# A PEER layer kernel: top 16 of two token blocks made later, and gathered v rows of one block kept to five buffers

## The chip, the cores and the metric

The kernel runs on one core of a Trainium2 chip. A core has five engines that run side by side, each with its own instruction queue that is worked off in order: PE (TensorE, matmuls), DVE (VectorE), ACT (ScalarE), POOL (GpSimd, here the issuer of gathers) and SP (SyncE, here the issuer of plain transfers). The metric is device time in microseconds (us) of one launch.

## The reference

One layer on 1024 tokens of width 1024: attention and a gated MLP, whose output is added to x, then a PEER layer, and a last RMSNorm. The change touches PEER only:

```python
q = (xb @ w_q).reshape(PEER_TOKEN_BLOCK, PEER_HEADS, 2, PEER_HALF)
s = jnp.einsum('thpd,hpnd->thpn', q, sub_keys).astype(jnp.float32)
vals, idx = lax.top_k(s, K)                     # best 16 of 128 keys, per head and half
cand = vals[:, :, 0, :, None] + vals[:, :, 1, None, :]
best, flat = lax.top_k(cand.reshape(..., K * K), K)   # best 16 of 256 pairs
...
expert = i1 * PEER_KEYS + i2                    # one of 16384
g = jax.nn.softmax(best, axis=-1)
h = jnp.einsum('thkd,td->thk', w_u[expert], xb)
a = (g * jax.nn.gelu(h)).astype(xb.dtype)
return jnp.einsum('thk,thkd->td', a, w_v[expert])
```

With 8 heads and 16 picks a token uses 128 of 16384 experts.

## The kernel before

The tokens are eight blocks of 128. **The front**, up to some 1291 us, runs attention, MLP and the PEER query for pairs of blocks (the stages of PLAN). Its last stage S of a pair multiplies the queries by the keys (PE, 128x512 scores per block and c, tile ss, in PSUM) and `top` takes the best 16 of each 128 scores on DVE: MAX, MAX_INDEX, MATCH_REPLACE, MAX, MAX_INDEX (L565 to L569), 16 such units a block and four rows of scores each. `select(b)` takes the best 16 pairs, the expert numbers and the softmax, on DVE (scratch tiles sf, sb, so).

PEER itself is done in two ways. **Blocks 0, 1, 6, 7** gather: for each of 128 picks POOL issues an indirect transfer of one 128x1024 tile of rows (`fetch`, L664), of w_u (DVE takes the product sum, L685) and then of w_v (DVE adds to y, L699). I call these u rows and v rows, and v0 or v7 the v rows of block 0 or 7. The tiles come from gat (five buffers) and, for the names in MIXED, from gat2 (three) where a running count modulo 8 is 5 or more. gat2 exists only once the front's pools are closed; selects 6 and 7 (LATE) are emitted inside the dense stage and take their scratch from gat2.

**Blocks 2 to 5** are dense. In `gates` the 128 picks become a matrix over all experts: DVE makes one-hots oh2 (L626), ACT oh1 (L645, L646), PE multiplies them (pgg, L650), ACT copies to st (L651), SP writes st to DRAM (gd, L652). G1 is for blocks 2 and 3, G2 for 4 and 5. The **dense stage** then reads tokens (xl, L724, split in xh and xl by ACT L726 and DVE L727), gates gg (L750) and weights ur and vr (L757, L777), and runs 32 groups of 4 x 128 experts: PE hp (L765 to L767), gelu, y (L743 to L745). ACT and DVE split ur, vr and a into high and low parts (uh, ul; vh, vl; ah, al). Part of the output is summed in PSUM; for the rest DVE adds op to dacc twice a group (L791). The first group is group 0.

A scheduler puts the instructions of all this into one fixed order per engine when the kernel is built; gathered rows of blocks 0, 1, 6, 7 are spread between the other work, and what is not placed by the end of the dense stage comes after it.

Of the kernel before, what the change touches and what calls it, by code (L numbers as in the profile page):

```python
# [7 lines left out]
F32 = mybir.dt.float32  # L8
# [4 lines left out]
AF = mybir.ActivationFunctionType  # L13
# [5 lines left out]
P = 128  # L19
D = 1024  # L20
# [7 lines left out]
NPAIR = PH * K  # L28
# [14 lines left out]
FRONT_POOL = 1.0  # L43
WS = 3
G1B = (2, 3)
G1 = dict(st=1, o1=2, o2=3, gt=1)
G2 = dict(st=3, o1=4, o2=4, gt=2)
PLAN = "A0:34 A0:01g2 B0 Y0 D0 S0 X t0 u0 t1 A1:34201 A2:20134 M1 B1 Y1 D1 S1 A3:01234 B2 M2 t2 t3 Y2 M3 D2 B3 S2 t4 t5 G1 Y3 Z G2 D3 S3"
SEQ = "d u1 v0 v1 u6 v6 u7 v7"
LATE = {2: 6, 6: 7}  # L50
# [2 lines left out]
X4 = 2  # L53
UG = {3: 3, 4: 2}
WP = 3
MIXED = "v1 u6 v6 u7 v7"
OH2 = "d"
OH1 = "a"
TCK = dict(schedule_with_timeline_sim=True)
# [2 lines left out]
def peer_block(tc, d):  # L62
# [3 lines left out]
    with ExitStack() as ctx:  # L66
# [162 lines left out]
        def front():  # L229
# [300 lines left out]
            def stage_s(p):  # L530

                blocks = PASSES[p]
                for b in blocks:
                    vi = vip.tile([P, 2, PH, 2, K], F32, name=f"vi{b}", tag="vi")
                    S["vi", b] = (vi[:, 0], vi[:, 1].bitcast(U32))
                T = S["sT", p]
                nt = len(blocks) * P

                def query(c):

                    kt = f2.tile([P, 4, P], F32, name=f"kt{p}_{c}", tag="kt")
                    sp.dma_start(kt, d["keys"][:, c * 4:(c + 1) * 4, :])
                    ps = [accp.tile([P, 512], F32, name=f"pq{p}_{c}_{i}", tag="acc") for i in range(2)]
                    src = lambda q: d["w_q"][:, q * 2:q * 2 + 2, c * 512:(c + 1) * 512]
                    for dc, w in pieces(src, f"sc{p}_{c}", T[1] is None):
                        for q in range(4):
                            mm(ps[q // 2][:, (q % 2) * nt:(q % 2) * nt + nt], cut(w, slice(None), slice(q * P, (q + 1) * P)),
                               cut(T, slice(None), dc, slice(0, nt)), dc == 0 and q % 2 == 0, dc == DC - 1, skip_group_check=True)
                    qT = f2.tile([P, 4, PW * P], F32, name=f"sq{p}_{c}", tag="sq")
                    for q in range(0, 4, 2):  # L550
                        act.activation(qT[:, q:q + 2, :nt], ps[q // 2][:, :2 * nt].rearrange("p (a b) -> p a b", a=2), AF.Copy)
                    return kt, qT

                def top(c, kt, qT):
                    for i, b in enumerate(blocks):
                        vals, idxs = S["vi", b]
                        ps = accp.tile([P, 512], F32, name=f"ss{b}_{c}", tag="acc")
                        for q in range(4):
                            pe.matmul(ps[:, q * P:(q + 1) * P], qT[:, q, at(i)], kt[:, q, :], start=True, stop=True)
                        for q in range(4):  # L560
                            h, hf = (c * 4 + q) // 2, q % 2
                            s_ = ps[:, q * P:(q + 1) * P]
                            v_, i_ = vals[:, h, hf, :], idxs[:, h, hf, :]
                            rep = sm.tile([P, P], F32, name=f"rep{b}_{c}_{q}", tag="rep", bufs=2)
                            dve.max(v_[:, 0:8], s_)  # L565
                            dve.max_index(i_[:, 0:8], v_[:, 0:8], s_)
                            dve.match_replace(rep, v_[:, 0:8], s_, -3e38)
                            dve.max(v_[:, 8:16], rep)
                            dve.max_index(i_[:, 8:16], v_[:, 8:16], rep)  # L569

                last = None
                for c in range(4):
                    cur = c, *query(c)
                    if last:
                        top(*last)
                    last = cur
                top(*last)
# [76 lines left out]

        ring = [0]

        def fetch(b, src, ix, nm):
            k_ = ring[0] % (GAT + GAT2)
            ring[0] += 1
            if f"{src[2]}{b}" in MIXED and k_ >= GAT:  # L660
                t = gat2.tile([P, D], F32, name=f"{nm}", tag="gat2")
            else:
                t = gat.tile([P, D], F32, name=f"{nm}", tag="gat")
# [6 lines left out]
        def gather_u(b):  # L670
# [10 lines left out]
            dve.scalar_tensor_tensor(xn, x1, rs2_t[b], gr, op0=ALU.mult, op1=ALU.mult)  # L681
            h = gxn.tile([P, n], F32, name=f"h{b}", tag="h")
            for j in range(n):
                t = fetch(b, "w_u", idx[:, j:j + 1], f"u{b}_{j}")
                dve.tensor_tensor_reduce(t, t, xn, 1.0, 0.0, ALU.mult, ALU.add, h[:, j:j + 1])  # L685
            a = gxn.tile([P, n], F32, name=f"a{b}", tag="a")
            act.activation(a, h, AF.Gelu_apprx_tanh)
# [3 lines left out]
        def gather_v(b):  # L691
# [17 lines left out]
        def dense():  # L709
# [37 lines left out]
            for gi in range(NG):  # L747
# [122 lines left out]
```

## Time and profile before

| what | us |
|---|---|
| median of 3 runs (lowest, highest) | 2804.43 (2799.83, 2818.26) |
| the profiled execution's own time | 2804.69 |
| its span | 2802.8 |
| busy: PE, DVE, ACT, POOL | 2457.4, 2339.8, 1165.0, 1506.5 |
| mean DMA rate over the span | 310 GB/s |

The span is what the profile shows from the first to the last instruction; the 1.9 us around it belong to the launch. PE is busy in 88% of the span, DVE in 83%, ACT in 42% and POOL in 54%. These are averages over a front with changing bounds, a long dense stage and a tail, and a change has to be read in the stage that it touches.

### The profile page before, as it was taken

What the parts mean: (1) busy time and instruction counts of PE and PEld (TensorE: products, weight loads), DVE (VectorE), ACT (ScalarE), POOL (GpSimd) and SP (SyncE); (2) the same over time, 40 slices, a digit from 0 to 9 for tenths busy, and PEclk for the clock granted to TensorE, in tenths of its full rate; (3) what the DMA queues carried; (4) which work ended last, traced back from release to release, by engine and by line L of the source; (5) the groups of instructions that cost most, each with busy time, mean ns of one, the idle gap of its engine ahead of it and who ended that gap; (6) DMA issues with size and microseconds to landing.
All of it is one profiled execution on the core that took longest, in us unless ns stands there. A gap on an engine that the chain in (4) does not pass through costs nothing.

```text
span 2802.8 us, 33721 instructions
## 1 busy us (share of the span) xinstructions
PE 2457.4 (88%) x10764; PEld 1931.3 (69%) x10764; DVE 2339.8 (83%) x4967; ACT 1165.0 (42%) x2573; POOL 1506.5 (54%) x1139
## 2 busy tenths in 40 slices
PE   6789997996689767795999999999999999999990
PEld 5576654753457455684878878888888878888880
DVE  3449876999879999779998888888898788888898
ACT  4554332225863789896222323223232222323310
POOL 5262654447653346510666566565565577555665
PEclk9789998997789767795999999999999999999995
DMA  5155999998899679966999989999999999999998
GB/s 175 53 177 170 347 366 351 344 333 316 308 351 334 222 261 359 362 223 210 320 372 353 342 315 373 335 351 330 351 329 348 335 338 359 330 345 345 330 324 321
DMA packets 316513, 869.56 MB, mean 310 GB/s; under 512 B 26032, under 2 KB 93744, under 8 KB 312240
## 3 DMA queue, kind: packets, MB, share of 16 engines
q0 software_dynamic: 149760, 545.33, 53.1%
q1 hardware_dynamic: 166576, 322.09, 33.2%
q8 instruction: 84, 1.38, 0.2%
q14 instruction: 93, 0.76, 0.1%
HBM read 823.28 MB, written 44.04 MB: 309 GB/s over the span
## 4 chain that ended last, share of the span: by engine, by line
PE 40%; issue 16%; DVE 16%; POOL 11%; DMA 10%; ACT 6%; SPq 0%; POOLq 0%; DVEq 0%; ACTq 0%
POOL v L664 9%; PE pq L309 4%; PE hp L765 4%; PE hp L767 4%; PE hp L766 4%; DVE u L685 4%; PE y L744 3%; PE y L743 3%; PE y L745 3%; PE wo L309 3%; DVE y L699 3%; DMA v<-in_w_v_dram,idx 2%; DMA u<-in_w_u_dram,idx 2%; ACT oh L646 2%; PE wi L309 2%
## 5 line engine op out<-in xcount | busy, mean ns | idle before, releaser
L664 POOL DMA_INDIRECT v<-in_w_v_dram,idx x512 | 687.1, 1342 | 618.2 <-DVE y L699 326.9
L664 POOL DMA_INDIRECT u<-in_w_u_dram,idx x512 | 695.6, 1359 | 528.0 <-DVE h L685 235.2
L699 DVE SCALAR_TENSOR_TENSOR y<-v,a,y 128x1024 f32<-128x1024 f32 x512 | 656.2, 1282 | 36.8 <-DMA v<-in_w_v_dram,idx 24.8
L685 DVE CUSTOM_DVE_ANT_0 u<-u,xn 128x1024 f32<-128x1024 f32 x512 | 615.0, 1219 | 41.6 <-DMA u<-in_w_u_dram,idx 41.0
L765 PE MATMUL hp<-xh,uh 128*128 128x512 f32 x1024 | 402.6, 393 | 32.2 <-ACT uh L760 22.2
L767 PE MATMUL hp<-xh,ul 128*128 128x512 f32 x1024 | 400.8, 392 | 2.6 <-DVE ul L761 2.6
L766 PE MATMUL hp<-xl,uh 128*128 128x512 f32 x1024 | 401.3, 392 | 0.0
L778 ACT ACTIVATE vh<-vr 128x1024 fp32r<-128x1024 f32 x128 | 131.5, 1052 | 503.7 <-PE op L745 485.3
L650 PE MATMUL pgg<-oh,oh 128*128 128x128 f32 x1024 | 219.7, 368 | 114.3 <-ACT st L651 69.3
L743 PE MATMUL y<-vh,ah 128*128 128x512 f32 x768 | 298.8, 389 | 0.0
L744 PE MATMUL y<-vl,ah 128*128 128x512 f32 x768 | 298.8, 389 | 0.0
L650 PEld LDWEIGHTS pgg<-oh,oh 128*128 128x128 f32 x1024 | 186.9, 261 | 158.4 <-ACT st L651 81.9
L745 PE MATMUL y<-vh,al 128*128 128x512 f32 x768 | 286.1, 390 | 2.9 <-DVE al L775 2.9
L765 PEld LDWEIGHTS hp<-xh,uh 128*128 128x128 f32 x1024 | 194.2, 190 | 75.9 <-ACT uh L760 23.3
L646 ACT ACTIVATE oh<-oh,gT 128x128 f32<-128x128 f32 x512 | 221.9, 512 | 16.3 <-DVE gT L613 16.3
L767 PEld LDWEIGHTS hp<-xh,ul 128*128 128x128 f32 x1024 | 193.8, 189 | 44.0 <-DVE ul L761 3.3
L766 PEld LDWEIGHTS hp<-xl,uh 128*128 128x128 f32 x1024 | 194.1, 190 | 40.0
L760 ACT ACTIVATE uh<-ur 128x1024 fp32r<-128x1024 f32 x128 | 135.3, 1057 | 177.8 <-PE hp L766 165.5
L309 PE MATMUL pq<-sT,sc 128*128 128x256 f32 x768 | 186.0, 392 | 2.0 <-ACT sT L127 2.0
L761 DVE TENSOR_TENSOR ul<-ur,uh 128x1024 fp32r<-128x1024 f32 x128 | 156.3, 1221 | 19.9 <-ACT uh L760 19.9
L645 ACT ACTIVATE oh<-iota,gT 128x128 f32<-128x128 f32 x512 | 168.7, 420 | 7.7 <-PE pgg L650 7.6
L309 PEld LDWEIGHTS pq<-sT,sc 128*128 128x128 f32 x768 | 144.3, 195 | 34.6 <-issue 9.2
(439 smaller groups left out, 4141.3 us busy)
## 6 DMA issues: line engine op xcount, KB each, us to landing
ur<-in_w_uT_dram SPq DMA_DIRECT2D x128, 512.0 KB, 6.6
vr<-in_w_v_dram SPq DMA_DIRECT2D x128, 512.0 KB, 6.3
wi<-in_w_in_dram SPq DMA_DIRECT2D x80, 512.0 KB, 5.4
sc<-in_w_q_dram SPq DMA_DIRECT2D x64, 512.0 KB, 5.8
gd<-st SPq DMA_DIRECT2D x32, 1024.0 KB, 6.7
gg<-gd SPq DMA_DIRECT2D x16, 2048.0 KB, 22.2
wo<-in_w_out_dram SPq DMA_DIRECT2D x32, 512.0 KB, 7.0
x<-in_x_dram SPq DMA_DIRECT2D x16, 512.0 KB, 5.8
```

Source lines behind the costliest of these rows:

```text
L309: pe.matmul(ps, s_[i], m_[j], start=first and n == 0, stop=last and n == len(ops) - 1, **kw)
L646: act.activation(oh1[:, j, :], oh1[:, j, :], AF.Relu, scale=gT[:, 3, t_ + j:t_ + j + 1], bias=gT[:, 2, t_ + j:t_ + j + 1])
L650: pe.matmul(pg[:, j * P:(j + 1) * P], oh2[:, j, :], oh1[:, j, :], start=True, stop=True)
L664: pool.indirect_dma_start(out=t, out_offset=None, in_=d[src], in_offset=bass.IndirectOffsetOnAxis(ap=ix, axis=0))
L685: dve.tensor_tensor_reduce(t, t, xn, 1.0, 0.0, ALU.mult, ALU.add, h[:, j:j + 1])
L699: dve.scalar_tensor_tensor(y, t, a[:, j:j + 1], y, op0=ALU.mult, op1=ALU.add)
L743: pe.matmul(ps, ah[:, bs], vh[:, hs], start=first, stop=False, skip_group_check=True)
L744: pe.matmul(ps, ah[:, bs], vl[:, hs], start=False, stop=False, skip_group_check=True)
L745: pe.matmul(ps, al[:, bs], vh[:, hs], start=False, stop=last, skip_group_check=True)
L765: pe.matmul(hp[:, :TD], uh[:, ds_], xh[:, dc, :], start=(dc == 0), stop=False)
L766: pe.matmul(hp[:, :TD], uh[:, ds_], xl[:, dc, :], start=False, stop=False)
L767: pe.matmul(hp[:, :TD], ul[:, ds_], xh[:, dc, :], start=False, stop=(dc == DC - 1))
```

## The change

Three things, and what follows from them for buffers:

1. MIXED gives each gathered stream a first pick from which it may use gat2. For v of block 1 it is 72, so v_0 to v_71 take only the five gat buffers, also where the count modulo 8 says gat2; the others are as before.
2. For blocks 6 and 7 `top` no longer takes the best 16. ACT copies the 128x512 scores to SBUF (tile ssb, one buffer), SP writes them to DRAM (ss_6 and ss_7). In the dense stage `late_top16` reads them back, 512 KB at a time, into gat2 tiles (s8), and takes the best 16 there, just ahead of `select`. Scratch for MATCH_REPLACE (sr) is a gat2 tile too.
3. The one-hots oh2 of G1 have two buffers rather than three.

```diff
--- before.py
+++ after.py
@@ -43,7 +43,7 @@
 FRONT_POOL = 1.0
 WS = 3
 G1B = (2, 3)
-G1 = dict(st=1, o1=2, o2=3, gt=1)
+G1 = dict(st=1, o1=2, o2=2, gt=1)
 G2 = dict(st=3, o1=4, o2=4, gt=2)
 PLAN = "A0:34 A0:01g2 B0 Y0 D0 S0 X t0 u0 t1 A1:34201 A2:20134 M1 B1 Y1 D1 S1 A3:01234 B2 M2 t2 t3 Y2 M3 D2 B3 S2 t4 t5 G1 Y3 Z G2 D3 S3"
 SEQ = "d u1 v0 v1 u6 v6 u7 v7"
@@ -53,7 +53,7 @@
 X4 = 2
 UG = {3: 3, 4: 2}
 WP = 3
-MIXED = "v1 u6 v6 u7 v7"
+MIXED = {"v1": 72, "u6": 0, "v6": 0, "u7": 0, "v7": 0}
 OH2 = "d"
 OH1 = "a"
 TCK = dict(schedule_with_timeline_sim=True)
@@ -132,9 +132,32 @@
 
         x1_d = [dram.tile([P, D], F32, name=f"x1_{b}") for b in range(NB)]
         gd = dram.tile([P, NTB, P, TB], F32, name="gd")
+        ss_d = {b: dram.tile([P, 4, 512], F32, name=f"ss_{b}") for b in LATE.values()}
         xT_d = dram.tile([P, DC, TD], F32, name="xT_d")
         sel_t = {}
         rs2_t = {}
+
+        def top16(b, c, s4, reps):
+
+            vals, idxs = S["vi", b]
+            for q in range(4):
+                h, hf = (c * 4 + q) // 2, q % 2
+                s_, rep = s4[:, q * P:(q + 1) * P], reps[q % 2]
+                v_, i_ = vals[:, h, hf, :], idxs[:, h, hf, :]
+                dve.max(v_[:, 0:8], s_)
+                dve.max_index(i_[:, 0:8], v_[:, 0:8], s_)
+                dve.match_replace(rep, v_[:, 0:8], s_, -3e38)
+                dve.max(v_[:, 8:16], rep)
+                dve.max_index(i_[:, 8:16], v_[:, 8:16], rep)
+
+        def late_top16(b):
+
+            w_ = gat2.tile([P, D], F32, name=f"sr{b}", tag="gat2")
+            for c in range(0, 4, 2):
+                s8 = gat2.tile([P, 2, 512], F32, name=f"s8{b}_{c}", tag="gat2")
+                sp.dma_start(s8, ss_d[b][:, c:c + 2, :])
+                for k_ in range(2):
+                    top16(b, c + k_, s8[:, k_, :], [w_[:, 0:P], w_[:, P:2 * P]])
 
         def select(b):
 
@@ -553,20 +576,16 @@
 
                 def top(c, kt, qT):
                     for i, b in enumerate(blocks):
-                        vals, idxs = S["vi", b]
                         ps = accp.tile([P, 512], F32, name=f"ss{b}_{c}", tag="acc")
                         for q in range(4):
                             pe.matmul(ps[:, q * P:(q + 1) * P], qT[:, q, at(i)], kt[:, q, :], start=True, stop=True)
-                        for q in range(4):
-                            h, hf = (c * 4 + q) // 2, q % 2
-                            s_ = ps[:, q * P:(q + 1) * P]
-                            v_, i_ = vals[:, h, hf, :], idxs[:, h, hf, :]
-                            rep = sm.tile([P, P], F32, name=f"rep{b}_{c}_{q}", tag="rep", bufs=2)
-                            dve.max(v_[:, 0:8], s_)
-                            dve.max_index(i_[:, 0:8], v_[:, 0:8], s_)
-                            dve.match_replace(rep, v_[:, 0:8], s_, -3e38)
-                            dve.max(v_[:, 8:16], rep)
-                            dve.max_index(i_[:, 8:16], v_[:, 8:16], rep)
+                        if b in LATE.values():
+                            sb = f2.tile([P, 512], F32, name=f"ssb{b}_{c}", tag="ssb", bufs=1)
+                            act.activation(sb, ps, AF.Copy)
+                            sp.dma_start(ss_d[b][:, c, :], sb)
+                        else:
+                            reps = [sm.tile([P, P], F32, name=f"rep{b}_{c}_{q}", tag="rep", bufs=2) for q in range(2)]
+                            top16(b, c, ps, reps)
 
                 last = None
                 for c in range(4):
@@ -654,10 +673,10 @@
 
         ring = [0]
 
-        def fetch(b, src, ix, nm):
+        def fetch(b, src, ix, nm, j):
             k_ = ring[0] % (GAT + GAT2)
             ring[0] += 1
-            if f"{src[2]}{b}" in MIXED and k_ >= GAT:
+            if j >= MIXED.get(f"{src[2]}{b}", NPAIR) and k_ >= GAT:
                 t = gat2.tile([P, D], F32, name=f"{nm}", tag="gat2")
             else:
                 t = gat.tile([P, D], F32, name=f"{nm}", tag="gat")
@@ -681,7 +700,7 @@
             dve.scalar_tensor_tensor(xn, x1, rs2_t[b], gr, op0=ALU.mult, op1=ALU.mult)
             h = gxn.tile([P, n], F32, name=f"h{b}", tag="h")
             for j in range(n):
-                t = fetch(b, "w_u", idx[:, j:j + 1], f"u{b}_{j}")
+                t = fetch(b, "w_u", idx[:, j:j + 1], f"u{b}_{j}", j)
                 dve.tensor_tensor_reduce(t, t, xn, 1.0, 0.0, ALU.mult, ALU.add, h[:, j:j + 1])
             a = gxn.tile([P, n], F32, name=f"a{b}", tag="a")
             act.activation(a, h, AF.Gelu_apprx_tanh)
@@ -695,7 +714,7 @@
             y = gxn.tile([P, D], F32, name=f"y{b}", tag="xn")
             pool.dma_start(y, x1_d[b])
             for j in range(n):
-                t = fetch(b, "w_v", idx[:, j:j + 1], f"v{b}_{j}")
+                t = fetch(b, "w_v", idx[:, j:j + 1], f"v{b}_{j}", j)
                 dve.scalar_tensor_tensor(y, t, a[:, j:j + 1], y, op0=ALU.mult, op1=ALU.add)
             ms = smg.tile([P, 2], F32, name=f"msg_{b}", tag="msg")
             jk = gxn.tile([P, D], BF16, name=f"jk3_{b}", tag="jk", bufs=1)
@@ -782,6 +801,7 @@
                     for o in stay:
                         product(kept[o], o, gi * GRP + k_, av[k_], gi + k_ == 0, gi == NG - 1 and k_ == GRP - 1)
                 if gi in LATE:
+                    late_top16(LATE[gi])
                     select(LATE[gi])
                 for o in turn:
                     op = hop.tile([P, 512], F32, name=f"op{gi}_{o[0]}_{o[1]}", tag="ho")
```

The order of the engines moves as follows. First **SP's queue, from the last gd on**. Before:

```order
L652 DMA gd<-st_8728 128x2048
L652 DMA gd<-st_8798 128x2048
L724 DMA xl<-xT_d 128x1024 x4
L735 DMA dacc_9467<-x_5_91 128x1024
L750 DMA gg_9475<-gd 128x32x128
L757 DMA ur_9479<-in_w_uT_dram 128x1024
L777 DMA vr_9517<-in_w_v_dram 128x1024
L757 DMA ur_9521<-in_w_uT_dram 128x1024
L777 DMA vr_9559<-in_w_v_dram 128x1024
```

and with the change (L671 is gd, L769 gg, L776 ur, L796 vr, L743 xl; L585 writes scores, L158 reads them back; tile numbers stand in the names):

```order
L769 DMA gg_9261<-gd 128x32x128
L776 DMA ur_9265<-in_w_uT_dram 128x1024
L796 DMA vr_9303<-in_w_v_dram 128x1024
L776 DMA ur_9307<-in_w_uT_dram 128x1024
L796 DMA vr_9345<-in_w_v_dram 128x1024
L769 DMA gg_9803<-gd 128x32x128
L585 DMA ss_95<-ssb_3_9189 128x512
L776 DMA ur_9349<-in_w_uT_dram 128x1024
L776 DMA ur_9391<-in_w_uT_dram 128x1024
L158 DMA s_2_10090<-ss_95 128x1024
L585 DMA ss_96<-ssb_3_9197 128x512
L743 DMA xl<-xT_d 128x1024 x4
```

xl stood directly behind the last gd; now two gg, four ur, two vr, two writes and one read of scores stand between.

**DVE, around the first one-hot of the last chunk of gates (oh_31_0).** Before, top16 of block 7 (L565 to L569) runs between the one-hots:

```order
L567 MATCH_REPLACE rep_3_2_9402<-vi_8993,ss_3_9385 128x128
L565 MAX vi_8993<-ss_3_9385 128x8
L569 MAX_INDEX vi_8993<-vi_8993,rep_3_1_9396 128x8
L626 TENSOR_TENSOR oh_31_0_8799<-gT_8297,iota 128x512
L568 MAX vi_8993<-rep_3_2_9402 128x8
L566 MAX_INDEX vi_8993<-vi_8993,ss_3_9385 128x8
L567 MATCH_REPLACE rep_3_3_9408<-vi_8993,ss_3_9385 128x128
L569 MAX_INDEX vi_8993<-vi_8993,rep_3_2_9402 128x8
```

and with the change v rows of block 1 (L718) run there, and top16 of block 6 from the scores read back (L147 on) follows the last one-hot:

```order
L718 SCALAR_TENSOR_TENSOR y_19127<-v_32_19225,a_18716,y_19127 128x1024
L718 SCALAR_TENSOR_TENSOR y_19127<-v_33_19228,a_18716,y_19127 128x1024
L645 TENSOR_TENSOR oh_31_0_8753<-gT_8251,iota 128x512
L645 TENSOR_TENSOR oh_31_4_8770<-gT_8251,iota 128x512
L718 SCALAR_TENSOR_TENSOR y_19127<-v_34_19231,a_18716,y_19127 128x1024
L645 TENSOR_TENSOR oh_31_8_8787<-gT_8251,iota 128x512
L718 SCALAR_TENSOR_TENSOR y_19127<-v_35_19234,a_18716,y_19127 128x1024
L718 SCALAR_TENSOR_TENSOR y_19127<-v_36_19237,a_18716,y_19127 128x1024
L645 TENSOR_TENSOR oh_31_12_8804<-gT_8251,iota 128x512
L147 MAX vi_8946<-s_0_10048 128x8 x6
L148 MAX_INDEX vi_8946<-vi_8946,s_0_10048 128x8
```

37 v rows of block 1 stand ahead of oh_31_12 now, 5 before.

**ACT, around the end of block 0** (jk is the sum of squares of its finished y). Before, jk stands behind the second half of the sixteen one-hots of chunk 24:

```order
L646 ACTIVATE oh_24_0_8310<-oh_24_0_8310,gT_8297 128x128 x4
L646 ACTIVATE oh_24_4_8327<-oh_24_4_8327,gT_8297 128x128 x4
L646 ACTIVATE oh_24_8_8344<-oh_24_8_8344,gT_8297 128x128 x4
L646 ACTIVATE oh_24_12_8361<-oh_24_12_8361,gT_8297 128x128 x4
L551 ACTIVATE sq_0_9038<-pq_0_1_8997 128x512
L687 ACT_TABLE_LOAD
L687 ACTIVATE a_18760<-h_18375 128x128
L702 ACTIVATE jk_0_19150,msg_19149<-y_18763 128x1024
L651 ACTIVATE st_8308<-pgg_0_8320 128x128x4
```

and with the change:

```order
L706 ACT_TABLE_LOAD
L706 ACTIVATE a_18716<-h_18331 128x128
L721 ACTIVATE jk_0_19106,msg_19105<-y_18719 128x1024
L670 ACTIVATE st_8181<-pgg_8_8227 128x128x4
...
L665 ACTIVATE oh_24_0_8264<-oh_24_0_8264,gT_8251 128x128 x4
L665 ACTIVATE oh_24_4_8281<-oh_24_4_8281,gT_8251 128x128 x4
L665 ACTIVATE oh_24_8_8298<-oh_24_8_8298,gT_8251 128x128 x4
L665 ACTIVATE oh_24_12_8315<-oh_24_12_8315,gT_8251 128x128 x4
L670 ACTIVATE st_8262<-pgg_0_8274 128x128x4
```

jk moved ahead of these sixteen, and of their first halves.

## Rows read from the trace of the kernel before

**Rows 1.** windows: us from:to, length, busy us per engine, granted clock, DMA share, GB/s
```profile
core 0: us, PE busy (x) PEld busy (x) DVE busy (x) ACT busy (x) POOL busy (x), PEclk, DMA share, GB/s
1200.00:1250.00 50.00, 50.00 (x303) 45.78 (x302) 32.06 (x123) 50.00 (x141) 8.98 (x7) 1.00 0.70 252
1300.00:1350.00 50.00, 34.48 (x134) 27.29 (x135) 46.27 (x113) 18.44 (x25) 10.49 (x7) 0.77 0.90 297
1400.00:2700.00 1300.00, 1287.09 (x5652) 1062.74 (x5651) 1114.95 (x1364) 372.62 (x476) 798.84 (x558) 1.00 0.94 344
2700.00:2802.00 102.00, 32.33 (x143) 26.46 (x141) 92.87 (x104) 11.68 (x19) 57.76 (x51) 0.68 0.85 314
```

**Rows 2.** timeline, DVE: start us, duration us, engine, line, operation, tiles, count, idle before
```profile
1188.20 1.28 DVE L699 SCALAR_TENSOR_TENSOR y<-v,a,y 128x1024 f32<-128x1024 f32 x1 [0.55 <-DMA v<-in_w_v_dram,idx]
...
1280.98 0.68 DVE L626 TENSOR_TENSOR oh<-gT,iota 128x512 f32<-128x512 f32 x1
...
1364.50 0.68 DVE L791 TENSOR_TENSOR dacc<-dacc,op 128x512 f32<-128x512 f32 x1
...
2732.77 0.68 DVE L791 TENSOR_TENSOR dacc<-dacc,op 128x512 f32<-128x512 f32 x1
...
2768.95 25.05 DVE L699 SCALAR_TENSOR_TENSOR y<-v,a,y 128x1024 f32<-128x1024 f32 x19
```

**Rows 3.** waits of PE, 1350 to 2740: total us, times, longest
```profile
PE hp L765 <- DVE dacc L791: 8.0, 3, 3.8
PE y L745 <- DVE al L775: 2.9, 4, 1.1
```

**Rows 4.** timeline, ACT: last gates
```profile
1185.66 6.26 ACT L646 ACTIVATE oh<-oh,gT 128x128 f32<-128x128 f32 x16 [4.99 <-DVE gT L613]
...
1193.93 1.04 ACT L702 ACTIVATE jk<-y 128x1024 bf16<-128x1024 f32 x1
...
1290.75 0.60 ACT L651 ACTIVATE st<-pgg 128x512 f32<-128x512 f32 x1 [0.45 <-PE pgg L650]
```

**Rows 5.** timeline, POOL: v rows
```profile
1225.97 1.41 POOL L664 DMA_INDIRECT v<-in_w_v_dram,idx  x1 [0.30 <-issue]
1330.02 1.69 POOL L664 DMA_INDIRECT v<-in_w_v_dram,idx  x1 [102.63 <-ACT vh L778]
```

**Rows 6.** timeline, SP's queue: loads issued at the start of the dense stage
```profile
1291.38 0.32 SPq L652 DMA_DIRECT2D gd<-st  x1
1291.80 3.06 SPq L724 DMA_DIRECT2D xl<-xT_d  x4
...
1296.43 0.59 SPq L750 DMA_DIRECT2D gg<-gd  x1
1297.07 9.26 SPq L757 DMA_DIRECT2D ur<-in_w_uT_dram  x1
...
1307.86 0.56 SPq L750 DMA_DIRECT2D gg<-gd  x1
```

**Rows 7.** timeline, PE: first dense matmuls
```profile
1311.90 0.80 PE L765 MATMUL hp<-xh,uh 128*128 128x512 f32 x1 [21.18 <-ACT uh L760]
...
1317.96 0.80 PE L767 MATMUL hp<-xh,ul 128*128 128x512 f32 x1 [2.55 <-DVE ul L761]
```

**Rows 8.** groups by line, DVE, 1000 to 1290: busy us, mean ns, idle before
```profile
L565 DVE MAX8 vi<-ss 128x8 f32<-128x128 f32 x32 | 9.2, 293 | 1.1 <-PE ss L559 1.1
...
L568 DVE MAX8 vi<-rep 128x8 f32<-128x128 f32 x32 | 9.0, 283 | 0.0
```

**Rows 9.** one line's instructions: L551 (ACT copy from PSUM) and L626 (DVE one-hots)
```profile
L551 ACT ACTIVATE sq<-pq x8: 572/602/652, 1180.1 to 1253.2; 128x512 f32<-128x512 f32 x8
...
  PE pgg L650: 20.8, 14
```

**Rows 10.** DMA issues, 1290 to 1400: count, KB each, median us to landing
```profile
gg<-gd SPq DMA_DIRECT2D x3, 2048.0 KB, 13.6
...
xl<-xT_d SPq DMA_DIRECT2D x4, 512.0 KB, 7.4
```

## The prediction, made before the changed kernel ran

> **What bounds the kernel now.** I read the windows first [rows 1]. [...] After 2700 DVE is busy 92.87 of 102 us and PE is done. So the time is made of three pieces: when the dense stage gets under way, 32 expert groups of constant length, and a DVE tail. The DVE timeline gives the marks [rows 2]: the last one-hot of the gates at 1280.98, the second dacc of group 0 at 1364.50, the last dacc at 2732.77. Between the two daccs lie 31 groups: (2732.77 - 1364.50)/31 = 44.1 us each. In all of that PE waits only 8.0 us for dacc and 2.9 for al [rows 3], so nothing that DVE does between 1365 and 2732 shortens it, as long as it stays below 44 us a group. What is left after 2732.77 is 39 rows of v7 on DVE; 19 of them in a row take 25.05 us, 1.32 each [rows 2].
>
> What ends the stage ahead is ACT: its timeline [rows 4] shows jk of block 0 at 1193.93 and the last st at 1290.75, which ends at 1291.35 (I call this **t0**). The ACT rows between them come to 96.7 us of the 97.4 that pass, and the windows have ACT busy 50.00 of 50 from 1200 to 1250. DVE has 18 us free there [rows 1], and POOL stands still for 102.63 us, to 1330.02 [rows 5]: its queue is at v_5, the first v1 row for a gat2 buffer, and those hold the scratch of selects 6 and 7. After t0, SP's queue [rows 6] issues the last gd, xl at once, then dacc, gg at 1296.43, and a ur that is held 9.26 us. PE starts at 1311.90 and runs without a gap from 1317.96 [rows 7]: t0 + 26.6.
>
> **The change, part by part.** *v1 in the five gat buffers up to row 72.* POOL issues v1 rows in order and the 102.63 us stall goes. This pays nothing by itself, since POOL is not what ends the stage. It lets DVE run 37 v1 rows ahead of the last one-hot, where 5 stood, and 77 ahead of the second dacc of group 0, where 20 stood. At the end of group 3 the lead is only 93 against 79, because groups 1 and 2 now hold no v row at all: top16 and the selects fill them. The lead of 14 rows is what reaches the tail in the end: **27 v7 rows instead of 39 stand behind the last dacc**, 12 x 1.32 = **-15.8 us**, with no cover, since only DVE works there. Bounds: 12 x 1.20 = -14.4 (interleaved rows start 1.20 apart) and down to 0 only if the tail's gathers come late, for which 19 rows in 25.05 us leave no sign.
>
> *The DVE work between the last one-hot and the second dacc of group 0.* Counted in both orders, at the start-to-start durations of the same instructions. Before: 116 select rows 38.2 us, 15 v1 rows 18.9, 26 dense rows 20.9 and small ones, 79.5 in all; 83.5 passed, so waits were 4. After: 41 select rows 7.2, 80 top16 rows (16 units of five, one block, 1.19 each with their loads) 19.1, 40 v1 rows 49.2, dense rows the same, 97.5. So **+18.0 us** on a chain in which DVE is busy nearly all the time. The remaining selects and the top16 of block 7 lie in groups 1 to 3: 38.8, 42.2 and 41.9 us of DVE by the same count, below PE's 44.1, so they cost nothing while PE is the bound; were that cover thinner by 10 us a group, they would cost about 20 us.
>
> *Top16 from SBUF instead of PSUM.* The 128-wide MAX8 takes 293 ns from the PSUM scores and 283 ns from the SBUF copy rep [rows 8]; I price it as equal. [...]
>
> *The end of the gates (t0).* ACT gains five of the eight score copies inside this piece: a 128x512 from PSUM takes 0.60 us listed [rows 9], about 2.4 us in sum at start-to-start times. And jk of block 0 now stands ahead of the sixteen oh_24 on ACT instead of behind them; the ACT rows from jk to the last st come to 113.6 us, against 96.7. jk needs the last v0 row, which ended at 1189.5 before [rows 2], its gathers being two us apart on POOL. If v0 ends as before, jk starts at 1190 and t0 is 1190 + 113.6 = 1303.6 (+12). ACT's 4.99 us of waiting at 1185.66 shows that there is slack just ahead; if v0 ends 14 us earlier, t0 is 1289.6 (-2). The DVE rows from the first to the last v0 row sum to 288 us, against 290, so v0 hardly ends earlier for DVE's sake; I take **+7** (bounds -2 and +12), nearer the late end, and leave 5 us for that slack.
>
> *SP's queue.* xl, without which no dense matmul can start, is moved from directly behind the last gd to behind two gg (4 MB), four ur, two vr, two score writes and one read of scores. The two writes are in a chain: ACT's copies share one buffer, so each waits for the landing of the write before. Issue of the second gg was at t0 + 16.5 [rows 6]; write, landing 6 to 8, copy, write, then xl: t0 + 27 to 31; xl lands 7.4 later [rows 10]; and DVE's order has the xl subtractions behind the top16 of the second read, so the first is at about t0 + 39 to 47. PE would run without a gap from there, against t0 + 26.6: +12 to +20 over t0. This lies beside the DVE term, not on top of it: +18 is inside it. For what the two add by waiting for one another I put **+1** (bounds 0 and +20, the upper end being four landings at 13 us, as gg's, rather than 8).
>
> *o2 from 3 to 2 in the first gates.* All one-hots on DVE waited 20.8 us for PE [rows 9], over both gate stages. Bounds 0 and +10, half of them once more for the half of the gates that has one buffer less; I take 0, since 14 waits among 128 one-hots say that three buffers were seldom all taken.
>
> **Sum.** The second dacc of group 0: 1364.5 + 7 + 18 + 1 = 1390.5 (+26). Then 31 x 44.1 as before, and -15.8. On the profiled execution's 2804.69: 2804.69 + 26 - 15.8 = **2815 us**; the median shown, 2804.43, is the same within 0.3. One per cent, what a measurement here can tell from no change, is 28 us.
>
> **Rivals.** (A) *Slower: the loads ahead of xl bite.* Gathers now run from 1230 to 1330, where POOL stood still, and share the DMA with 8 MB ahead of xl. For it: 1300 to 1350 had a DMA share of 0.90 already [rows 1], gg took 13.6 us to land, ur was held 9.26. Against it: 1200 to 1300 had spare DMA. Price: four landings (write, write, read, xl) at 13 instead of 8 us, +20: dacc at 1410, 2835 us. It decides once the first xl subtraction is later than t0 + 50. [...]
> (B) *Faster: the start is not late.* v0 ends some 12 us early on the relieved DVE, xl lands early, and v1 rows only fill DVE's 18 free us. Then t0 is unmoved, the second dacc comes at 1364 to 1368, and only the tail counts: 2789 to 2793. Against it: 18 us more DVE rows stand ahead of that dacc.
> (C) *Nothing: one delay is hidden*: v0 ends early, so that t0 stays, and part of the v1 rows ahead of the dacc fill the 4 us of waits and DVE's free time: dacc at 1380, and the tail gives it back: 2804.
> (D) *The rows stay late anyway*: with five buffers each gather waits for a DVE row, DVE's fixed order then waits on the gathers among the one-hots, and the gates end late by more than 12: about 2825.
>
> **Chances.** Forecast (2806 to 2823) 0.42; C (2797 to 2806) 0.15; A 0.20; B 0.13; D 0.10. The range that holds 8 in 10 reaches from B's lower end to somewhat past A: **2786 to 2842**. Faster than 2776 needs a gain in the front that no row shows: 0.06. Slower than 2833 takes most of A and a little of D: 0.18. Within 1%: 0.76.
>
> **What would show it.** Right: POOL's stall of 102.6 us gone; last st near 1298; xl issued 27 to 31 us after it; second dacc of group 0 at 1384 to 1397; 44.1 us a group; 27 v7 rows and some 54 us after the last dacc instead of 70. Wrong: groups 1 to 3 longer than 45 us (then DVE is the bound there), gather waits in the tail, or the first PE matmul less than t0 + 27.

## The result: slower by 0.7 per cent, and the profile after

The changed kernel takes 2825.58 us (median; 2815.05 to 2836.43, 15 runs) against 2807.04 (2798.95 to 2818.26, 15 runs): ratio **1.0072** [1.0056, 1.0087]. Forecast were 2815 and a range of 2786 to 2842. The profiled executions have spans of 2802.8 and 2822.2, so the trace accounts for +19.4 us.

The DVE timeline of the changed kernel, to be read beside [rows 2]; L645 is the one-hot, L780 ul, L147 top 16, L746 xl, L811 dacc, L718 a v row. The last field is the idle time before, and what ended it:

```profile
1278.72 0.69 DVE L645 TENSOR_TENSOR oh<-gT,iota 128x512 f32<-128x512 f32 x1 [1.28 <-PE pgg L669]
...
1321.81 1.23 DVE L780 TENSOR_TENSOR ul<-ur,uh 128x1024 fp32r<-128x1024 f32 x1 [11.29 <-ACT uh L779]
...
1338.97 1.26 DVE L147 MAX8 vi<-s 128x8 f32<-128x128 f32 x6 [6.99 <-DMA s<-ss]
...
1351.08 1.28 DVE L746 TENSOR_TENSOR xl<-xl,xh 128x512 fp32r<-128x512 f32 x2
...
1400.01 0.69 DVE L811 TENSOR_TENSOR dacc<-dacc,op 128x512 f32<-128x512 f32 x1
...
2769.73 0.68 DVE L811 TENSOR_TENSOR dacc<-dacc,op 128x512 f32<-128x512 f32 x1
```

The second dacc of group 0 moved from 1364.50 to 1400.01, +35.5. The 31 groups after it take 1369.7 instead of 1368.3, +1.4. The tail behind the last dacc is 52.5 instead of 70.0, -17.5, with 27 v7 rows. 35.5 + 1.4 - 17.5 = 19.4: the three pieces are the whole difference.

DVE from the last one-hot to that dacc, in the kernel before and then in the changed one (the columns are those of [rows 1]), and what DVE waited for there in the changed one (total us, times, longest):

```profile
1280.98:1364.50 83.52, 55.88 (x221) 44.45 (x222) 79.02 (x189) 31.66 (x53) 21.33 (x17) 0.75 0.83 283
1278.72:1400.01 121.29, 55.60 (x225) 44.46 (x226) 97.13 (x260) 33.98 (x64) 46.73 (x41) 0.70 0.92 324
```

```profile
DVE ul L780 <- ACT uh L779: 12.5, 2, 11.3
DVE vi L147 <- DMA s<-ss: 7.0, 1, 7.0
DVE y L718 <- DMA v<-in_w_v_dram,idx: 4.1, 3, 2.7
```

ACT, beside [rows 4] (L721 is jk, L670 the last st, L584 a copy of scores):

```profile
1177.98 1.04 ACT L721 ACTIVATE jk<-y 128x1024 bf16<-128x1024 f32 x1
...
1291.29 0.60 ACT L670 ACTIVATE st<-pgg 128x512 f32<-128x512 f32 x1 [0.49 <-PE pgg L669]
...
1331.52 0.60 ACT L584 ACTIVATE ssb<-ss 128x512 f32<-128x512 f32 x1 [7.28 <-DMA ss<-ssb]
```

So t0 is 1291.89, where it was. What is late stands behind it in SP's queue, beside [rows 6] (L671 gd, L769 gg, L776 ur, L585 a score write, L743 xl; the second number is how long the issue took):

```profile
1291.91 0.32 SPq L671 DMA_DIRECT2D gd<-st  x1
1294.45 0.32 SPq L585 DMA_DIRECT2D ss<-ssb  x1
1300.16 0.59 SPq L769 DMA_DIRECT2D gg<-gd  x1
1300.80 13.88 SPq L776 DMA_DIRECT2D ur<-in_w_uT_dram  x1
...
1317.09 0.56 SPq L769 DMA_DIRECT2D gg<-gd  x1
1317.69 9.59 SPq L585 DMA_DIRECT2D ss<-ssb  x1
...
1332.14 0.33 SPq L585 DMA_DIRECT2D ss<-ssb  x1
1332.52 2.15 SPq L743 DMA_DIRECT2D xl<-xT_d  x4
```

Twelve transfers stand between the last gd and xl: the eleven listed with the change, and a score write at 1294.45, directly behind the gd, that the list does not show.

POOL, PE, one window and two landings, beside [rows 5], [rows 7], [rows 1] and [rows 10]:

```profile
1310.79 0.94 POOL L683 DMA_INDIRECT v<-in_w_v_dram,idx  x1 [2.15 <-DVE y L718]
1326.96 1.86 POOL L683 DMA_INDIRECT v<-in_w_v_dram,idx  x1 [15.23 <-DVE y L718]
```

```profile
1343.92 1.22 PE L784 MATMUL hp<-xh,uh 128*128 128x512 f32 x2 [52.67 <-ACT xh L745]
1351.81 0.80 PE L785 MATMUL hp<-xl,uh 128*128 128x512 f32 x1 [6.68 <-DVE xl L746]
```

```profile
core 0: us, PE busy (x) PEld busy (x) DVE busy (x) ACT busy (x) POOL busy (x), PEclk, DMA share, GB/s
1300.00:1350.00 50.00, 1.22 (x2) 0.50 (x2) 26.43 (x56) 9.91 (x14) 15.16 (x13) 0.50 1.05 385
```

```profile
gg<-gd SPq DMA_DIRECT2D x2, 2048.0 KB, 16.3
...
xl<-xT_d SPq DMA_DIRECT2D x4, 512.0 KB, 12.1
```

The 102.63 us of POOL are gone. From 1300 to 1350 PE now works 1.2 of 50 us and DVE 26.4, while the DMA share is 1.05 (385 GB/s), where it was 0.90 (297 GB/s). xl is issued at t0 + 40.6, lands in 12.1 us, not 7.4, and its first subtraction comes at t0 + 59.2, not t0 + 10.1. On DVE the xl subtraction stands behind most of the second top 16 (from 1338.97), for which DVE had waited for the scores read back. From 1351.8 PE runs without a wait of over 0.8 us to the second dacc.

### The profile page after: what moved, and what is told of

It is laid out like the page before. It is cut to its first block, busy times and chain, and to the rows that moved or that the text cites. A ratio compares the mean times of both kernels' runs of the same rounds, so it can differ in the third digit from the quotient of the medians.

```text
span 2822.2 us, 33738 instructions
## 1 busy us (share of the span) xinstructions
PE 2450.8 (87%) x10764; PEld 1928.4 (68%) x10764; DVE 2340.9 (83%) x4967; ACT 1171.2 (41%) x2583; POOL 1501.3 (53%) x1139
## 4 chain that ended last, share of the span: by engine, by line
PE 56%; DVE 15%; DMA 11%; issue 8%; ACT 7%; POOL 3%; SPq 1%; POOLq 0%; DVEq 0%; ACTq 0%
PE hp L784 7%; PE hp L785 7%; PE hp L786 7%; PE y L764 5%; PE y L762 5%; PE y L763 5%; PE pq L332 5%; DVE u L704 4%; DMA u<-in_w_u_dram,idx 3%; DMA v<-in_w_v_dram,idx 3%; PE wo L332 3%; ACT oh L665 2%; DVE y L718 2%; PE wi L332 2%; ACT oh L664 2%
## 5 line engine op out<-in xcount | busy, mean ns | idle before, releaser
L683 POOL DMA_INDIRECT v<-in_w_v_dram,idx x512 | 674.7, 1318 | 653.9 <-DVE y L718 329.6
L683 POOL DMA_INDIRECT u<-in_w_u_dram,idx x512 | 702.8, 1373 | 517.2 <-DVE h L704 228.9
L718 DVE SCALAR_TENSOR_TENSOR y<-v,a,y 128x1024 f32<-128x1024 f32 x512 | 656.3, 1282 | 52.3 <-DMA v<-in_w_v_dram,idx 45.4
L669 PE MATMUL pgg<-oh,oh 128*128 128x128 f32 x1024 | 210.4, 363 | 110.8 <-ACT st L670 64.5
L780 DVE TENSOR_TENSOR ul<-ur,uh 128x1024 fp32r<-128x1024 f32 x128 | 156.6, 1223 | 43.7 <-ACT uh L779 43.7
L793 ACT ACTIVATE ah<-ga 128x512 fp32r<-128x512 f32 x128 | 80.8, 631 | 217.2 <-DVE ga L790 217.1
```

The costliest lines, as they stand in the source:

```text
L669: pe.matmul(pg[:, j * P:(j + 1) * P], oh2[:, j, :], oh1[:, j, :], start=True, stop=True)
L683: pool.indirect_dma_start(out=t, out_offset=None, in_=d[src], in_offset=bass.IndirectOffsetOnAxis(ap=ix, axis=0))
```

## The experiments

Three theories of the late start: (1) the place of xl in SP's queue, (2) gathers that now share the DMA with the first loads, (3) DVE's rows ahead of the second dacc. All runs by their profiled execution; "rows" are v7 rows behind the last dacc, the last column is the ratio of times to the kernel before. t0 alone varies from 1285.7 to 1297.7 over these single executions, so marks are read from t0. In all fourteen the second dacc comes 46 to 53 us behind the end of PE's last wait of over 3 us ahead of it (its wait for the first dense matmul, or a later one): what holds PE's first dense matmuls up moves that dacc.

| kernel | t0 | first xl, after t0 | second dacc | 31 groups | tail (rows) | ratio [95%] |
|---|---|---|---|---|---|---|
| before | 1291.4 | 10.1 | 1364.5 | 1368.3 | 70.0 (39) | 1 |
| changed | 1291.9 | 59.2 | 1400.0 | 1369.7 | 52.5 (27) | 1.0072 [1.0056, 1.0087] |
| e1 | 1290.4 | 25.2 | 1382.1 | 1355.0 | 38.0 (15) | 0.9892 [0.9867, 0.9916] |
| e2 | 1288.7 | 11.4 | 1362.7 | 1350.3 | 115.7 (73) | 1.0102 [1.0075, 1.0129] |
| e3 | 1290.4 | 7.7 | 1362.1 | 1356.3 | 88.6 (53) | 1.0014 [0.9997, 1.003] |
| e4 | 1289.1 | 22.0 | 1377.3 | 1361.8 | 64.1 (35) | 1.0009 [0.9991, 1.0027] |
| e5 | 1295.4 | 35.6 | 1380.3 | 1370.2 | 87.0 (53) | 1.0096 [1.0063, 1.0129] |
| e6 | 1285.7 | 22.3 | 1369.6 | 1371.0 | 47.5 (23) | 0.9931 [0.9908, 0.9954] |
| e7 | 1290.5 | 24.8 | 1381.4 | 1373.6 | 37.6 (16) | 0.9949 [0.9929, 0.9969] |
| e8 | 1286.8 | 20.6 | 1373.7 | 1380.6 | 36.6 (15) | 0.9961 [0.9939, 0.9983] |
| e9 | 1297.1 | 24.0 | 1386.8 | 1364.0 | 36.7 (15) | 0.9918 [0.9892, 0.9943] |
| e10 | 1288.4 | 24.9 | 1372.2 | 1367.7 | 36.8 (15) | 0.9908 [0.9883, 0.9933] |
| e11 | 1297.7 | 26.8 | 1389.6 | 1362.5 | 37.9 (15) | 0.9922 [0.9896, 0.9947] |
| e12 | 1293.6 | 24.7 | 1373.2 | 1367.8 | 35.6 (14) | 0.9891 [0.9873, 0.9909] |

**The parts alone.** e1 is the kernel before with the first part:

```diff
-MIXED = "v1 u6 v6 u7 v7"
+MIXED = {"v1": 72, "u6": 0, "v6": 0, "u7": 0, "v7": 0}
-            if f"{src[2]}{b}" in MIXED and k_ >= GAT:
+            if j >= MIXED.get(f"{src[2]}{b}", NPAIR) and k_ >= GAT:
```

> The kernel before with the first part of the change alone: v rows of block 1 keep to the five gat buffers up to the 73rd; top 16 of blocks 6 and 7 stays in the front, o2 has three buffers. In its order xl stands directly behind the last gd again, 29 v1 rows stand ahead of the last one-hot, 56 ahead of the second dacc of group 0, and 15 v7 rows behind the last dacc (39 before, 27 with the whole change). Theory 1 (the dense start of the changed kernel was late because of the loads and score writes ahead of xl in SP's queue): xl is issued within 2 us of the last gd, the second dacc of group 0 comes at 1364 to 1376, and the tail is 24 rows x 1.32 = 31.7 us shorter: 2773 to 2785 us. Theory 2 (it was late because gathers now share the DMA with those loads, wherever they stand): xl lands late all the same, second dacc at 1385 to 1395, 2794 to 2804. Theory 3 (DVE's row count ahead of the dacc is what delays it): 36 more v1 rows at 1.20 less 18 us that DVE had free is +25, second dacc near 1390, 2798.

2778.16 us. The time is theory 1's, the marks are not: the dacc came at 1382, late by 17.6, and the 31 groups gave back 13.3. DVE's waits from the last one-hot to that dacc are 4.0 us in all, so there it is busy (91.0 us, 79.0 before); ACT and SP of e1 (L220 is the exp of a select, L757 ur, L760 uh):

```profile
1330.79 0.31 ACT L220 ACTIVATE g<-g 128x128 f32<-128x128 f32 x1 [20.27 <-DVE g L219]
1331.01 1.04 ACT L760 ACTIVATE uh<-ur 128x1024 fp32r<-128x1024 f32 x1
```

```profile
1298.04 0.58 SPq L750 DMA_DIRECT2D gg<-gd  x1
1298.67 22.27 SPq L757 DMA_DIRECT2D ur<-in_w_uT_dram  x1
```

uh waits behind an exp for DVE's select, so DVE's rows (theory 3) hold PE's start here. ur is held 22 us, not 9 (theory 2); whether that would hold PE up by itself is tried in e9 to e12.

e2 is the changed kernel with `"v1": 0`:

> The changed kernel with the first part undone: v rows of block 1 may use gat2 from the first on; top 16 of blocks 6 and 7 is late, o2 has two buffers. In its order xl stands directly behind the last gd, 5 v1 rows ahead of the last one-hot and of the second dacc of group 0, 73 v7 rows behind the last dacc. Theory 1: xl is not late, second dacc at 1355 to 1370, tail 34 rows x 1.32 = 45 us longer than before: 2840 to 2855. Theory 2: few gathers run there, so the same. Theory 3: DVE has top 16 of both blocks (38 us) ahead of that dacc instead of 15 v1 rows and the selects, so second dacc no later than 1364: 2840 to 2850. All agree that top 16 made late, alone, costs some 40 us; what would speak against the counting of rows is a time within 15 us of before.

2836.87 us; dacc and tail as all theories said.

e3 is the kernel before with `G1 = dict(..., o2=2, ...)`:

> The kernel before with two buffers instead of three for the one-hots oh2 of the first gates, nothing else. I had priced this at 0 (bounds 0 and +10) through waits of the one-hots. In its order 53 v7 rows stand behind the last dacc instead of 39, and 12 instead of 20 v1 rows ahead of the second dacc of group 0. If rows behind the last dacc are what sets the end: 14 x 1.32 = +18, 2820 to 2826. If the one-hots' waits are the whole cost: 2804 to 2815, with longer waits for PE at the one-hots between 670 and 900.

2814.02 us, not told from no change. The tail has its +18.6, but the dacc comes 2.4 earlier and the 31 groups take 12.0 less: the count of rows behind the last dacc sets the tail, and not by itself the time. jk came at 1174.90 here, at 1194.34 in e1: with the second buffer less, block 0 ends early.

**Place or contention.** e4 gives ssb memory that the dense stage does not take over:

```diff
-sb = f2.tile([P, 512], F32, name=f"ssb{b}_{c}", tag="ssb", bufs=1)
+sb = vip.tile([P, 512], F32, name=f"ssb{b}_{c}", tag="ssb", bufs=1)
```

> The changed kernel with the copy of the scores (ssb) in a pool that lives through the whole kernel, instead of one whose memory the dense stage takes over; all else as in the changed kernel. In its order xl stands one score write behind the last gd, not twelve transfers; 66 v1 rows stand ahead of the second dacc of group 0 (77 in the changed kernel) and 35 v7 rows behind the last dacc (27). Theory 1 (place in SP's queue): first xl subtraction within t0 + 15 instead of t0 + 59, DVE's waits of 25 us between the last one-hot and that dacc fall under 10, second dacc at 1365 to 1380, and with 4 rows less than before in the tail 2800 to 2815. Theory 2 (DMA share of the gathers): xl lands in 12 us as in the changed kernel, the ur and gg behind it come late, waits stay near 20, second dacc at 1385 to 1395, 2820 to 2830. Theory 3 (DVE's rows): 11 v1 rows less, 13 us less, second dacc near 1387, 2822.

2808.09 us. xl is issued 1.9 us after the last gd, PE runs from t0 + 37.3 instead of t0 + 59.9, and the dacc comes 22.7 us earlier than in the changed kernel: place counts. It changes in SP's queue and in DVE's order at once, since xl no longer stands behind the second top 16 either; the two were not tried apart. Theory 1's other marks failed. xl still lands in 12.0 us, and its first subtraction is at t0 + 22, not within 15. DVE's idle time up to the dacc is 23.6 us, as in the changed kernel (24.2); what fell is its busy time, from 97.1 to 77.7. DVE and SP of e4:

```profile
1309.90 1.28 DVE L718 SCALAR_TENSOR_TENSOR y<-v,a,y 128x1024 f32<-128x1024 f32 x1 [1.20 <-DMA v<-in_w_v_dram,idx]
1311.10 4.90 DVE L746 TENSOR_TENSOR xl<-xl,xh 128x512 fp32r<-128x512 f32 x8
```

```profile
1291.11 4.51 SPq L743 DMA_DIRECT2D xl<-xT_d  x4
...
1299.25 20.58 SPq L585 DMA_DIRECT2D ss<-ssb  x1
1319.92 0.38 SPq L776 DMA_DIRECT2D ur<-in_w_uT_dram  x1
```

ACT has the first xh at t0 + 12.6, but on DVE v rows stand ahead of the subtractions, and they wait for their gathers. PE's start then waits for ur, which stands behind a score write that was held 20.58 us.

e5 is the changed kernel with `"v1": 32`: the twelve transfers stay ahead of xl, the gathers go.

> The changed kernel with the first pick of block 1 that may use gat2 at 32 instead of 72; top 16 stays late. Its order keeps the same twelve transfers between the last gd and xl, but POOL has only 37 v1 rows to gather before it stands still for gat2, so that few gathers run from 1291 to 1350; 37 v1 rows stand ahead of the second dacc of group 0 (77 in the changed kernel), 53 v7 rows behind the last dacc (27). Theory 2 (in the changed kernel the gathers' share of the DMA made the loads late): with the gathers gone xl lands as in the kernel before (8 us, not 12), the ur behind the first gg is held about 9 us, not 14, and the first xl subtraction comes at t0 + 35 to t0 + 45 instead of t0 + 59. Theory 1 (their place behind one another in the queue, write after landing of write): t0 + 52 or later whatever the gathers do. Time in either case: second dacc 1375 to 1390, 31 groups of 44, tail 53 rows, some 88 us: 2822 to 2842.

SP of e5, and its window:

```profile
1299.26 0.59 SPq L769 DMA_DIRECT2D gg<-gd  x1
1299.89 5.62 SPq L776 DMA_DIRECT2D ur<-in_w_uT_dram  x1
...
1319.88 2.31 SPq L743 DMA_DIRECT2D xl<-xT_d  x4
```

```profile
1300.00:1350.00 50.00, 19.48 (x71) 15.10 (x72) 29.28 (x122) 16.38 (x22) 0.00 (x0) 0.63 0.82 275
```

2836.66 us. The first ur is held 5.62 us, not 13.88, xl is issued at t0 + 24.5, and the first subtraction comes at t0 + 35.6. Of the 49.1 us by which it is later in the changed kernel than before, 23.6 go when the gathers go, and 25.5 are left with the twelve transfers ahead of xl. The split is not a clean one, and 23.6 is an upper figure for the gathers: of the same twelve transfers one score write now stands ahead of the second gg, which brings xl forward too, and with the gathers go all v rows of DVE between the last one-hot and the dacc (40 in the changed kernel). 18.9 of the 23.6 us lie ahead of the first xh on ACT (t0 + 51.3 and t0 + 32.4), the other 4.7 in DVE's rows between that xh and the subtraction. Both theories have a share; how large each is stays open.

**Where the gain of the rows goes.** e6 and e7 are e1 with 32 and 48, e8 is e4 with 128 (never gat2):

> The first part alone as in the run of the rows alone, with the first pick that may use gat2 at 32 instead of 72. In its order 37 v1 rows stand ahead of the second dacc of group 0 (56 with 72), 23 v7 rows behind the last dacc (15). The rows alone had DVE without a wait over 2.8 us in all from the last one-hot to that dacc, which came at 1382. If DVE's rows set that dacc: 19 rows x 1.20 = 23 us less, down to the floor of 1362 to 1366 that the loads allow; tail +8 x 1.32 = +10.6: 2766 to 2774, faster than the rows alone. If the load of the DMA by gathers sets it: a little less gain, dacc 1368 to 1375, 2774 to 2784. Each holds for 31 groups of 43.7 us; stalls of PE for dacc can add up to 13 us.

> As the run before, with 48. In its order 53 v1 rows ahead of the second dacc of group 0, 16 v7 rows behind the last dacc. If DVE's rows set that dacc: 3 rows less than with 72, dacc near 1379, tail +1.3 us: 2772 to 2780, as the rows alone.

> The changed kernel with ssb in a pool of its own place, as in the run above with that edit, and v1 rows that never use gat2. In its order xl stands one score write behind the last gd; 66 v1 rows ahead of the second dacc of group 0 as there, 82 and 95 ahead of those of groups 1 and 2 (77 and 77 there), 15 v7 rows behind the last dacc (35 there). If rows behind the last dacc set the end and groups 1 to 3 stay under PE's 44 us on DVE: dacc 1377, tail 20 rows x 1.32 = 26 us shorter: 2774 to 2786. If groups 1 to 3 become bound by DVE through selects, top 16 and v1 rows together: 10 to 20 us of that is lost, 2787 to 2800.

2789.76, 2794.03 and 2796.47 us, all slower than e1, and all by the 31 groups: e7 has e1's dacc and tail within 1 us, and 18.6 us more between. I had taken that piece as fixed. In e8 it is 18.8 us more than in e4, the amount that the second expectation gave, but not where it gave it: groups 1 to 3 take 139.2 us there against 136.9 in e4, and the rest is lost in later groups.

**e1's start.** e9 ties the exp of selects 6 and 7 to group 2 and group 6; e10 ties their first step to groups 1 and 3, with 128 for 72:

```diff
+z = smd.tile([P, 1], F32, name=f"hold{gi}", tag="hold")
+act.activation(z, ga[:, 0, 0:1], AF.Copy, scale=0.0)
-act.activation(g, g, AF.Exp)
+act.activation(g, g, AF.Exp, bias=z)                  # e9
+dve.tensor_scalar(vals, vals, z, None, ALU.add)       # e10
```

> The rows alone (gat2 from the 73rd v1 row), with the exp of selects 6 and 7 tied to group 2 and group 6: its bias is zero times a gelu output of that group, so that ACT cannot have it ahead of the first uh of the dense stage. Its order keeps 56 v1 rows ahead of the second dacc of group 0 and 15 v7 rows behind the last dacc. In the rows alone ACT waited 20.27 us at that exp for DVE's select and turned to the first uh only at 1331; PE started at 1332 and the second dacc came 48 to 50 us later, as in every run so far (47 to 51). If the exp held PE up: uh at the landing of the first ur, 1325 or so, PE at 1326, dacc at 1374 to 1377, 5 to 8 us less than the rows alone on these marks; time 2765 to 2775 if PE's stalls in the 31 groups stay at 4 us, up to 2790 if they come to 17 us and the slow clock. If the loads (DMA shared with gathers, first ur held 22 us) are the bound: PE at 1330 or later, no change.

> The rows alone with v1 never in gat2, and all of selects 6 and 7 tied to groups 1 and 3 (zero times a gelu output is added to their scores), so that none of the select stands ahead of the first matmuls. In its order 59 v1 rows ahead of the second dacc of group 0, 15 v7 rows behind the last dacc. If DVE's select and the exp behind it set PE's start: PE at 1322 to 1327, second dacc at 1368 to 1375. If the loads do: PE at 1330 or later, second dacc at 1378 or later. Groups 1 to 4 then hold more DVE work (two selects, 25 us each): with PE stalls of 5 us 2762 to 2772, with 17 us and the slow clock after them 2775 to 2788.

2783.27 and 2779.71 us. In e9 uh starts at t0 + 36.3 (t0 + 40.7 in e1), as soon as ur has landed, but ul then waits for DVE: the exp had held uh up by 4 us, and the dacc is 2 us earlier from t0. In e10 PE runs from t0 + 37.0 and the dacc comes at t0 + 83.8 (91.8 in e1): without the select ahead of it, and with 128 for 72, that is 8 us. What PE's start waits for there is uh, and uh for ur. e11 and e12 are e1 and e10 with the first two ur issued ahead of gg:

```diff
+pre = [d2.tile([P, D], F32, name=f"ur{e}", tag="ur") for e in range(2)]
+for e in range(2):
+    sp.dma_start(pre[e], d["w_uT"][e])
```

> The rows alone with the first two ur loads issued ahead of the first gg (2 MB) instead of behind it; all else, 56 v1 rows ahead of the second dacc of group 0 and 15 v7 rows behind the last dacc, as in the rows alone. There the first ur was held 22 us in the queue behind gg and PE started at t0 + 42. If gg with the gathers beside it is what holds ur: uh at t0 + 16 to t0 + 22, PE starts at t0 + 25 to t0 + 32 (the xl subtractions on DVE, t0 + 25, are next in line), but the third ur still stands behind both gg, so the second dacc gains 5 to 10 us only: 1372 to 1378, 2768 to 2776 with the stalls of the rows alone in the 31 groups, up to 2788 with more of them. If DVE's select is the bound there: PE as late as before.

> The kernel with the selects held, with the same two ur loads ahead of the first gg. Its order has 59 v1 rows ahead of the second dacc of group 0, 14 v7 rows behind the last dacc. There uh waited for ur until t0 + 36, and PE ran from t0 + 37. If the load of ur is the bound: PE starts at t0 + 18 to t0 + 26, may stop for the third ur (behind both gg) until t0 + 43, second dacc at 1362 to 1368 with t0 near 1288, 2766 to 2774. If not: no change, 2778 to 2782.

2787.42 and 2777.11 us. PE starts at t0 + 23.7 and t0 + 24.2. In e11 it then waits 10.69 us for ul, and the dacc is at t0 + 91.9, no gain: DVE, busy with the select, v rows and the xl subtractions, is the next bound. In e12 it is at t0 + 79.6, 4 us better than e10. Its ratio is e1's within the intervals; e1, one part of the change alone, is as fast as anything tried, some 1.1% faster than the kernel before. No kernel tried brings the dacc back to where it was from t0 with v1 rows in five buffers (79.6 at best, 73.1 before).

## Why the prediction was right, point by point

- **Direction and range** held; the point was 9 us low in the profiled execution (+19.4, not +10). The second dacc is where it was missed: +35.5, not +26. Most signs of being right that depend on the start failed: the last st did not move, xl was issued 40.6 us after it and not 27 to 31, the dacc came at 1400 and not by 1397. The stall of POOL, the 27 rows and the tail came as said.
- **The start of PE** is the term that was mis-sized. I gave SP's queue +12 to +20 us on PE's start (t0 + 39 to 47) and laid it inside DVE's 18. PE ran with no wait over 0.8 us from t0 + 59.9 instead of t0 + 26.6, +33.3. With t0 (+0.5) and the stretch from there to the dacc (48.2 us instead of 46.5, +1.7) that is the 35.5.
- **Tail** -15.8: measured -17.5, with the 27 rows counted.
- **t0** +7: measured +0.5. The ACT rows from jk on were right (1177.98 + 113.6 = 1291.6). Wrong was where block 0 ends: its last v row ended at 1177.7, not 1189.5. I had let the third part of the change count for nothing but one-hots' waits; alone, it has jk at 1174.90 (e3). In all kernels here with two such buffers jk starts at 1172.6 to 1181.5, in all with three at 1188.9 to 1201.9. Why is open.
- **DVE's rows** +18: from the last one-hot to the dacc DVE is busy 97.1 us instead of 79.0, +18.1; counted were 97.5 and 79.5. The count was right. That it sets the dacc was not shown: behind the first xl subtraction PE has no wait of over 0.8 us up to its last op of group 0, and DVE adds that op as it comes. The rows count ahead of the xl subtractions, where PE waits for them.
- **Waits** +1, bounds 0 and +20: DVE is idle 24.2 us there instead of 4.5, +19.7. This is the same miss as PE's start, seen from DVE, and it is rival A's price. Its mark, a first xl subtraction later than t0 + 50, came true (59.2). In the working I let the loads lie inside DVE's 18 us; DVE worked its rows off in order (gathers issued from 1302.89 to 1310.79 landed within 11.5 us, and their five v rows ran from 1325.41, behind the ul for which DVE stood 11.29 us), so what it waits for at ul (12.5) and at the second top 16 (7.0) adds to its rows ahead of the xl subtractions instead. With the last one-hot, 2.3 us earlier, rows and waits make the 35.5 once more. A's 2835 was not reached mainly because the 7 us for t0 did not come.
- **Rival B** was half true: block 0 ended 12 us early and t0 stayed; but xl did not come early. Rival D is out: the gates did not end late. C had t0 right too, but its dacc (1380) did not come.
- **31 groups** "as before" came out at +1.4 us by chance: over these kernels they vary from 1350.3 to 1380.6, so they are not of constant length. A sign of being wrong came true: groups 1 to 3 took 49.2, 42.8 and 49.6 us, 7.4 more than before in sum, and later groups took 6.0 less. DVE's sums per group were right (busy 38.7, 41.8 and 42.0 us; counted 38.8, 42.2 and 41.9), but DVE waited too, and PE then for dacc. DVE and PE of the changed kernel, 1400 to 1542 us (total us, times, longest):

```profile
DVE vi L147 <- DMA s<-ss: 7.7, 1, 7.7
DVE y L718 <- DMA v<-in_w_v_dram,idx: 7.1, 5, 2.9
```

```profile
PE hp L784 <- DVE dacc L811: 6.7, 2, 3.7
```

- **Top 16 from SBUF** at no cost: MAX8 takes 281 ns from the scores read back, 293 ns from PSUM before [rows 8]. Right.
- **The parts do not add up.** The dacc: rows alone +17.6, late alone (with the two buffers of oh2) -1.8, together +35.5; in e2 no gathers meet the score chain, in e1 no score chain stands ahead of xl. The same ur was held 13.88 us in the changed kernel, with gathers beside it, and 5.62 in e5, where POOL was busy 0.00 us from 1300 to 1350. It was held without gathers too: 9.20 us in e2, with xl just ahead.

## What to carry to other kernels

A queue that stands still may be doing others a favour: before a stall is taken out, look at what the freed transfers will meet, here the first loads of the next stage, with the DMA's share at 1.05. Where an engine works its rows off in order, as DVE did here, add the waits for late loads to its rows; do not lay one beside the other. Count the rows only up to the one that the next engine waits for, here the xl subtraction. And run the parts of a change apart: here one part alone was worth -1.1%, and the whole cost +0.7%.

## What the runs showed of the hardware that was not expected

A short wait of PE can cost more than itself. PE in the kernel before, at 2294 us (start, duration):

```profile
2294.44 0.80 PE L765 MATMUL hp<-xh,uh 128*128 128x512 f32 x1 [3.85 <-DVE dacc L791]
2295.03 0.63 PE L766 MATMUL hp<-xl,uh 128*128 128x512 f32 x1
...
2298.87 0.63 PE L766 MATMUL hp<-xl,uh 128*128 128x512 f32 x1
2299.30 0.55 PE L767 MATMUL hp<-xh,ul 128*128 128x512 f32 x1
2299.69 0.39 PE L765 MATMUL hp<-xh,uh 128*128 128x512 f32 x1
```

After 3.85 us of waiting the matmuls start 0.43 us apart for 5 us, at a granted clock of 0.50 (2294.4 to 2299.5), and then 0.23 apart, at 1.00 (2300 to 2302): some 2.4 us on top of the wait. In e1 PE waits for dacc too:

```profile
PE hp L765 <- DVE dacc L791: 5.7, 5, 2.0
```

Its longest wait there is 2.0 us, and no 10 us of its 31 groups show a granted clock below 1.00. But the length of a wait does not decide it. PE in e9, twice:

```profile
1477.34 0.50 PE L765 MATMUL hp<-xh,uh 128*128 128x512 f32 x1 [2.59 <-DVE dacc L793]
1477.68 0.40 PE L766 MATMUL hp<-xl,uh 128*128 128x512 f32 x1
```

```profile
1567.34 0.50 PE L765 MATMUL hp<-xh,uh 128*128 128x512 f32 x1 [1.95 <-DVE dacc L793]
...
1569.03 0.63 PE L765 MATMUL hp<-xh,uh 128*128 128x512 f32 x1
```

The matmul behind the wait of 2.59 us is listed with 0.40 us. Behind the wait of 1.95 us matmuls are slow from 1568.6 to 1572.0, with 0.63 us listed, as at the clock of 0.50 above, and so they are in the kernel before behind one of 2.60 us at 1453.39. Which waits are followed by the lower clock was not found out.

Summing PE's idle time and the time that the slow clock took (one minus the granted clock, over windows of 10 us) gives 13.4 + 5.1 in the kernel before, 12.1 + 6.8 in the changed one, 4.3 + 0 in e1, 2.1 + 0 in e2 and 21.1 + 6.8 in e8. Take these off the 31 groups, and 1348 to 1353 us are left in each of the fourteen kernels of the table. The spread of that piece, 30 us, is more than the whole change; which v rows of a group make dacc late was not tried.
